# Two transformer blocks on one core: another way to sum the modulation over the partitions

## The chip, the cores and the metric

The kernel runs on one core of a Trainium2 chip. The metric is device time in microseconds (us) of one execution, the median of several; lower is better. A core has a matmul engine (TensorE, PE in the profile), three elementwise engines (VectorE or DVE, ScalarE or ACT, GpSimd or POOL), and queues that start DMAs; here nearly all of them are issued on the queue of SyncE (SP), in the order of the program. Every engine works through its own instructions in order and waits for the others by semaphores.

## What is computed

Two transformer blocks on 256 tokens of width 1024, in float32. The first is a mixer (gated convolution and forgetting attention) and a SwiGLU layer. The second has two layers, each an attention and a SwiGLU layer, and each of the four is wrapped in a modulation that is worked out from one vector `c`:

```python
c_act = silu(c)                               # 1 x 1024
for i in range(2):
    mod = c_act @ ada_w[i] + ada_b[i]         # 1024 x 6144
    sh_a, sc_a, g_a, sh_f, sc_f, g_f = split(mod, 6)
    h = rms_norm(x, norm_g[i, 0]) * (1 + sc_a) + sh_a
    y = attention_i(h)
    x = x + g_a * rms_norm(y, norm_g[i, 1])
    h = rms_norm(x, norm_g[i, 2]) * (1 + sc_f) + sh_f
    x = x + g_f * rms_norm(swiglu(h), norm_g[i, 3])
```

The change concerns the last step of `c_act @ ada_w[i]` alone: twelve vectors of 1024 values.

## The kernel before

All 256 tokens stay in the core's on-chip memory, and 227 MB of weights stream through it once. A weight tile of 128x512 is split into two parts (`hi`, a rounded copy written by ScalarE, and `lo`, the rest, written by VectorE, in `fill`, lines 331 to 360), and each product of weights and tokens is three matmuls (`triple`, lines 385 to 395): hi by hi, hi by lo, lo by hi. Weights arrive in 3 buffers `raw` of 1 MB each; split tiles wait in 16 pairs (`slots`), and in the SwiGLU layers in 8 more (`wp`). Each split tile of a SwiGLU layer feeds 6 matmuls.

The order of all instructions on each engine is written out when the program is built. `Order` (line 111) is a small planner: it keeps a clock `now` that advances with each matmul (`mm`, `tr`), and lanes for the other engines with estimated costs (`Lane`, line 77). Side work is written as generators that are spawned and resumed when the planner's clock reaches the time that they yielded. `pin` (line 127) then fixes each engine's order. Real waits are by semaphores, so an instruction whose input comes later than planned holds up all that is behind it on its engine or queue.

The modulation is side work of this kind. `ada` (lines 659 to 690) goes through 12 vectors (`ada_order`) in two halves `cc` of 512 columns, 4 loads of 512 KB each (`araw`). For each half, 8 VectorE instructions multiply a 128x512 tile of weights by a value per partition and add it to a tile `asum` (2 buffers), which also gets the bias in its first row. What is then left is a sum over the 128 partitions, by `ada_finish` (lines 626 to 657), in one of two ways:

- Shifts and scales (`sh`, `sc`; 8 vectors, 16 halves) are wanted with the channel on the partition, as `fm`. PE turns the tile in four 128x128 pieces, VectorE sums each row out of PSUM (`reduce_sum`, 512 values per partition); for a scale a second small VectorE instruction adds 1 and multiplies by the norm's gain.
- Gates (`g`; 4 vectors, 8 halves) are wanted on all partitions, as a row of 1024. Before, a tile `gain` is loaded with the norm's gain, the same row on all partitions (`load_gain`). The sum is split into hi and lo (ScalarE, VectorE), two matmuls with a matrix of ones give it on all partitions, and VectorE multiplies `gain` by it. There are 2 `gain` tiles, shared with the norms of the first block; `ada_finish` waits until its tile has been loaded, and holds its `asum` until then.

The users are `chain` (line 555: it waits for `gb.marks`, the gate, and `ready`, shift and scale) and `evacuate`. At the start, `rows` (line 447) loads the small vectors as rows into one tile, each by a DMA of its own on SP, after the loads of `x` and the first weights and ahead of all further weights (lines 483 to 490); `turn_rows` turns them all by one PE instruction into the tile `cols`. `small` allocates one tile each; `pad_end` is one that nothing reads.

Of the kernel before, what the change touches and what calls it, by code (L numbers as in the profile page):

```python
# [12 lines left out]
F32 = mybir.dt.float32  # L13
F32R = mybir.dt.float32r
AF = mybir.ActivationFunctionType
OP = mybir.AluOpType
AX = mybir.AxisListType
# [3 lines left out]
P = 128  # L21
D = 1024
# [11 lines left out]
STOCK = 9  # L34
ADA_START, ADA_EARLY, ADA_LATE = 30.0, 5.5, 8.0
HEADS_1, HEADS_2 = 9.0, 2.0
PAD_END = 104
FIRST_DMA, SLOW_BYTES = 1.9, 2.2e6
RATE, SLOW_RATE = 360e3, 270e3
WARM = 6  # L40
# [178 lines left out]
def block_kernel(ctx: ExitStack, tc: tile.TileContext, a: dict, onehot: bass.AP, out: bass.AP):  # L219
    nc = tc.nc  # L220
    o = Order(tc)
    A, V, G = o.A, o.V, o.G
# [4 lines left out]
    dram = ctx.enter_context(tc.tile_pool(name="dram", bufs=1, space=DRAM))  # L227

    def ring(pool, name, n, shape, dtype=F32):
        return Ring([pool.tile(shape, dtype, name=f"{name}{i}") for i in range(n)])  # L230

    def small(name, shape, dtype=F32):
        return cst.tile(shape, dtype, name=name)

    banks = ring(psum, "bank", 8, [P, 512])
    raws = ring(cst, "raw", 3, [P, 2048])
    araws = ring(cst, "araw", 2, [P, 1024])
    slots = Ring([(small(f"hi{i}", [P, 512], F32R), small(f"lo{i}", [P, 512], F32R)) for i in range(16)])
    st = ring(cst, "st", 4, [P, 528])
    ch = ring(cst, "ch", 3, [P, 512])  # L240
    ep = ring(cst, "ep", 4, [P, 384])
    gains = ring(cst, "gain", 2, [P, D])
    asum = ring(cst, "asum", 2, [P, 512])
    junk = small("junk", [P, 512], mybir.dt.bfloat16)
    tiny = [small(f"tiny{i}", [P, 4]) for i in range(40)]
    tiny_at = [0]

    def tiny_tile():
# [113 lines left out]
    def split(hi, lo, src, after=0.0):  # L362
        t = A.activation(hi, src, AF.Copy, after=after)
        return V.tensor_sub(lo, src, hi.bitcast(F32), after=t)
# [80 lines left out]
    vec = {}  # L445
# [29 lines left out]
    def stay_warm():  # L475

        b = banks.take()
        for _ in range(WARM):
# [8 lines left out]
    later = rows(("c", a["c_2"].rearrange("l (k p) -> (l k) p", p=P), 8),  # L487
                 ("conv", a["conv_w"].rearrange("l t (k p) -> (l t k) p", p=P), 12),
                 ("ffn_pre", a["norm_ffn_pre"].rearrange("l (k p) -> (l k) p", p=P), 8),
                 *((("g", l, i), a["norm_g_2"][l, i].rearrange("(k p) -> k p", p=P), 8) for l in range(2) for i in (0, 2)))  # L490
    ident = small("ident", [P, P])
    make_identity(nc, ident)
    tri = small("tri", [P, P])
    nc.vector.memset(tri, 1.0)
    ones_r = small("ones_r", [P, P], F32R)
# [114 lines left out]
    def load_gain(src, gain):  # L610
        gain.tile = yield from o.get(gains)
        gain.load.t = o.dma(gain.tile, src.to_broadcast([P, D]))


    fm = [small(f"fm{l}", [P, 4, 8]) for l in range(2)]
# [3 lines left out]
    ada_done = {one: [Mark(), Mark()] for one in ada_order}  # L619
    gated = {one: Gain() for one in ada_order if one[1][0] == "g"}  # L620
# [2 lines left out]
    c_mark = Mark()  # L623
    c_act = small("c_act", [P, 8])

    def ada_finish(l, what, cc, sums, r):
        yield r
        c = slice(cc * 512, (cc + 1) * 512)
        if what[0] == "g":
            yield from o.until(gated[l, what].load)  # L630
            pair = yield from o.get(slots)
            hv, lv = pair
            r = split(hv, lv, sums)
            asum.give(sums, r)
            yield r
            tp = yield from o.get(banks)
            o.mm(tp, ones_r, hv, True, False)
            r = o.mm(tp, ones_r, lv, False, True)
            slots.give(pair, r)
            yield r  # L640
            dst = gated[l, what].tile[:, c]
            r = V.tensor_mul(dst, dst, tp)
        else:
            tp = yield from o.get(banks)
            for j in range(4):
                r = o.tr(tp[:, j * P:(j + 1) * P], sums[:, j * P:(j + 1) * P], ident)
            asum.give(sums, r)
            yield r
            i = {"sh_a": 0, "sc_a": 1, "sh_f": 2, "sc_f": 3}[what]
            dst = fm[l][:, i, cc * 4:cc * 4 + 4]  # L650
            r = V.reduce_sum(dst, tp.rearrange("p (k c) -> p k c", c=P), axis=AX.X)
            if what[1] == "c":
                yield r
                g = vec["g", l, 0 if what == "sc_a" else 2][:, cc * 4:cc * 4 + 4]
                r = V.scalar_tensor_tensor(dst, dst, 1.0, g, op0=OP.add, op1=OP.mult)
        banks.give(tp, r)
        ada_done[l, what][cc].t = r

    def ada():
        yield from o.until(c_mark)  # L660
        pieces = [(l, what, cc, k0) for l, what in ada_order for cc in range(2) for k0 in range(0, 8, 2)]
        loaded, t0 = [], o.now
        for i in range(len(pieces) + 1):
            if i < len(pieces):
                l, what, cc, k0 = pieces[i]
                c0 = parts_of.index(what) * D + cc * 512
                if k0 == 0:
                    if what[0] == "g" and cc == 0:
                        o.spawn(load_gain(a["norm_g_2"][l, 1 if what == "g_a" else 3].unsqueeze(0), gated[l, what]))
                    sums = yield from o.get(asum)  # L670
                    r = G.memset(sums, 0.0)
                    yield r
                    ba = o.dma(sums[0:1, :], a["ada_b_2"][l:l + 1, c0:c0 + 512])
                t = yield from o.get(araws)
                arrival = o.dma(t.rearrange("p (k c) -> p k c", c=512),
                                a["ada_w_2"][l].rearrange("(k p) c -> p k c", p=P)[:, k0:k0 + 2, c0:c0 + 512])
                loaded.append((l, what, cc, k0, t, max(arrival, ba), sums))
            if i:
                l, what, cc, k0, t, arrival, s = loaded.pop(0)
                yield max(arrival, t0 + i * ADA_EARLY)  # L680
                while (o.urgent or V.free > o.now + SLACK or
                       pos["lo"] - pos["first"] < STOCK and o.now < t0 + i * ADA_LATE):
                    yield o.now + 0.2
                for k in range(2):
                    r = V.scalar_tensor_tensor(s, t[:, k * 512:(k + 1) * 512], c_act[:, k0 + k:k0 + k + 1], s,
                                               op0=OP.mult, op1=OP.add)
                    yield r - 0.3
                araws.give(t, r)
                if k0 == 6:
                    o.spawn(ada_finish(l, what, cc, s, r), r)  # L690


    def scope(**kinds):

        stack, got = ExitStack(), {}
        for name, (n, shape, dtype) in kinds.items():
            got[name] = ring(stack.enter_context(tc.tile_pool(name=name, bufs=1, reuse_waits="tile")), name, n, shape, dtype)
        return stack, got
# [87 lines left out]
    cum, cum_mark = [small(f"cum{h}", [P, 8]) for h in range(2)], [Mark(), Mark()]  # L786
    rows_mark = Mark()

    small("pad_end", [P, PAD_END])
    phase, sc = scope(qp=(4, [P, 4, 256], F32), gp=(8, [P, 512], F32),  # L790
                                   mk=(1, [P, 256], F32))
    qks, gp = sc["qp"], sc["gp"]
# [209 lines left out]
    group(take(2), 260, keep_gb, None)  # L1002
    o.spawn(gates_of_c())
    o.spawn(ada(), ADA_START)
    group(take(2), 512, keep_gc, None)
    group(take(2), 512, make_z, None)
# [392 lines left out]
```

## Time and profile before

| | us |
|---|---|
| median of 3 runs (985.66 to 992.59) | 987.0 |
| the profiled execution, its own time | 987.64 |
| its span, first to last instruction | 985.9 |
| PE busy | 976.0 (99%) |
| VectorE busy | 739.6 (75%) |
| ScalarE busy | 605.1 (61%) |
| GpSimd busy | 35.4 (4%) |
| DMA queue of the weights, share of 16 engines | 67.9% |

The span is what the trace covers; 1.7 us of the execution lie around it. Durations of neighbouring instructions on one engine overlap in the records, on PE and on VectorE: what one more instruction costs its engine is the distance from start to start, not its duration.

### The profile page before, as it was taken

What the parts mean: (1) busy time and instruction counts of PE and PEld (TensorE: products, weight loads), DVE (VectorE), ACT (ScalarE), POOL (GpSimd) and SP (SyncE); (2) the same over time, 40 slices, a digit from 0 to 9 for tenths busy, and PEclk for the clock granted to TensorE, in tenths of its full rate; (3) what the DMA queues carried; (4) which work ended last, traced back from release to release, by engine and by line L of the source; (5) the groups of instructions that cost most, each with busy time, mean ns of one, the idle gap of its engine ahead of it and who ended that gap; (6) DMA issues with size and microseconds to landing.
All of it is one profiled execution on the core that took longest, in us unless ns stands there. A gap on an engine that the chain in (4) does not pass through costs nothing.

```text
span 985.9 us, 14069 instructions
## 1 busy us (share of the span) xinstructions
PE 976.0 (99%) x4826; PEld 805.9 (82%) x4826; DVE 739.6 (75%) x1470; ACT 605.1 (61%) x1286; POOL 35.4 (4%) x65
## 2 busy tenths in 40 slices
PE   9999999999999999999999999999999999999997
PEld 6888778888888878898888888888897888888885
DVE  6789789989888868887899888637766796464632
ACT  7756675765546437866775554537878785454631
POOL 1000000000000001000000000001000100000000
PEclk9999999999999999999999999999999999999999
DMA  7977777679988874784779989636542657556401
GB/s 244 345 240 263 258 281 238 232 226 344 349 279 303 300 272 170 270 297 153 243 223 324 349 287 322 224 106 222 180 137 82 198 196 261 200 166 206 161 22 44
DMA packets 143637, 227.22 MB, mean 230 GB/s; under 512 B 6087, under 2 KB 79028, under 8 KB 143564
## 3 DMA queue, kind: packets, MB, share of 16 engines
q1 hardware_dynamic: 143548, 226.30, 67.9%
q8 instruction: 38, 0.62, 0.3%
q14 instruction: 35, 0.29, 0.1%
q10 hardware_dynamic: 16, 0.00, 0.0%
HBM read 225.22 MB, written 2.63 MB: 231 GB/s over the span
## 4 chain that ended last, share of the span: by engine, by line
PE 90%; DMA 3%; DVE 3%; issue 2%; ACT 1%; SPq 0%; POOL 0%; DVEq 0%; POOLq 0%; ACTq 0%
PE bank L145 85%; PE bank L151 5%; DMA araw<-in_ada_w_dram 2%; DVE asum L89 1%; DVE lo L89 1%; DMA x<-in_x_dram 1%; DVE wp L89 0%; ACT hi L89 0%; SPq L137 0%; DMA raw<-in_w_in_dram 0%; DVE x L89 0%; DVE ch L89 0%; ACT junk L89 0%; POOL tiny L89 0%; ACT L89 0%
## 5 line engine op out<-in xcount | busy, mean ns | idle before, releaser
L89 DVE TENSOR_TENSOR lo<-raw,hi 128x512 fp32r<-128x512 f32 (+1 forms) x499 | 322.9, 677 | 35.8 <-ACT hi L89 34.1
L89 ACT ACTIVATE hi<-raw 128x512 fp32r<-128x512 f32 (+1 forms) x499 | 298.0, 621 | 59.8 <-PE bank L145 35.2
L145 PE MATMUL bank<-hi,hTh 128*128 128x512 f32 (+1 forms) x670 | 262.7, 392 | 0.5 <-ACT hTh L89 0.5
L145 PE MATMUL bank<-hi,hTl 128*128 128x512 f32 (+1 forms) x670 | 261.8, 391 | 0.2 <-DVE hTl L89 0.2
L145 PE MATMUL bank<-lo,hTh 128*128 128x512 f32 (+1 forms) x670 | 261.0, 389 | 0.0
L145 PE MATMUL bank<-hi,pair 128*128 128x512 f32 x528 | 173.5, 394 | 0.0
L89 DVE SCALAR_TENSOR_TENSOR asum<-araw,c_act,asum 128x512 f32<-128x512 f32 x192 | 143.3, 746 | 7.9 <-DMA araw<-in_ada_w_dram 7.2
L145 PEld LDWEIGHTS bank<-hi,hTl 128*128 128x128 f32 x670 | 125.9, 188 | 26.1 <-issue 1.3
L145 PEld LDWEIGHTS bank<-lo,hTh 128*128 128x128 f32 x670 | 126.0, 188 | 24.2 <-DVE lo L89 0.8
L145 PEld LDWEIGHTS bank<-hi,hTh 128*128 128x128 f32 x670 | 125.9, 188 | 24.2 <-ACT hTh L89 1.3
L145 PE MATMUL bank<-wp,hTh 128*128 128x512 f32 x388 | 120.4, 391 | 0.0
L145 PEld LDWEIGHTS bank<-hi,pair 128*128 128x128 f32 x528 | 98.0, 188 | 19.7 <-issue 0.2
L89 ACT ACTIVATE ep<-bank 128x256 f32<-128x256 f32 x66 | 25.4, 384 | 131.8 <-PE bank L145 131.3
L145 PE MATMUL bank<-lo,pair 128*128 128x512 f32 x264 | 103.6, 393 | 0.0
L89 ACT ACTIVATE wp<-raw 128x512 fp32r<-128x512 f32 x145 | 88.9, 630 | 22.4 <-PE bank L145 16.4
L89 DVE TENSOR_TENSOR wp<-raw,wp 128x512 fp32r<-128x512 f32 x145 | 95.2, 686 | 8.8 <-ACT wp L89 8.6
L145 PEld LDWEIGHTS bank<-wp,hTh 128*128 128x128 f32 x388 | 72.5, 188 | 15.1
L89 DVE TENSOR_TENSOR ep<-ep,bank 128x256 f32<-128x256 f32 x70 | 29.2, 417 | 66.7 <-ACT ep L89 66.4
L145 PE MATMUL bank<-wp,hTl 128*128 128x512 f32 x194 | 75.9, 391 | 0.0
L145 PE MATMUL bank<-wp,pair 128*128 128x512 f32 x288 | 75.8, 396 | 0.0
L145 PEld LDWEIGHTS bank<-wp,pair 128*128 128x128 f32 x288 | 53.0, 188 | 10.4
L89 DVE TENSOR_TENSOR pair<-bank,pair 128x256 fp32r<-128x256 f32 (+1 forms) x74 | 32.5, 439 | 37.3 <-ACT pair L89 36.7
(131 smaller groups left out, 953.6 us busy)
## 6 DMA issues: line engine op xcount, KB each, us to landing
araw<-in_ada_w_dram SPq DMA_DIRECT2D x96, 512.0 KB
raw<-in_ffn_w_in_dram SPq DMA_DIRECT2D x88, 512.0 KB
raw<-in_w_gate_up_dram SPq DMA_DIRECT2D x44, 512.0 KB
raw<-in_ffn_w_out_dram SPq DMA_DIRECT2D x22, 1024.0 KB
raw<-in_w_in_dram SPq DMA_DIRECT2D x16, 1024.0 KB
raw<-in_moba_w_qkv_dram SPq DMA_DIRECT2D x12, 1024.0 KB
raw<-in_diff_w_qkv_dram SPq DMA_DIRECT2D x12, 1024.0 KB
raw<-in_w_down_dram SPq DMA_DIRECT2D x11, 1024.0 KB
```

Source lines behind the costliest of these rows:

```text
L89: self.order.pin(self, fn(out, *args, **kw))
L145: self.pin(self.pe, self.nc.tensor.matmul(out, lhsT, rhs, start=start, stop=stop, skip_group_check=shared))
L151: self.pin(self.pe, self.nc.tensor.transpose(out, src, ident))
```

## The change

`ada_finish` no longer uses two ways. For each half, VectorE turns the 128x512 tile in blocks of 32x32 (`V.transpose`) into a tile `z`, and sums each row of each block (`reduce_sum`, 512 values per partition into 16), into one half of a tile `fold` of 128x32. After the second half, four float32 matmuls, with a stationary tile `stacked` of 128x32 (four 32x32 identities above each other) and 8 moving columns, give the vector's 1024 values as 128x8. For a shift VectorE copies them, for a scale it does the one instruction with 1 and the gain, for all 1024 values at once. For a gate it multiplies them by the norm's gain (128x8, loaded at the start with the other small vectors), the 128x8 go to DRAM by a DMA and come back on all partitions by another, into a `gain` tile that is only taken then. The gain loads ahead of a gate go. `tiny` has 36 instead of 40 buffers and `pad_end` goes.

```diff
-PAD_END = 104
-    tiny = [small(f"tiny{i}", [P, 4]) for i in range(40)]
+    tiny = [small(f"tiny{i}", [P, 4]) for i in range(36)]
...
-                 *((("g", l, i), a["norm_g_2"][l, i].rearrange("(k p) -> k p", p=P), 8) for l in range(2) for i in (0, 2)))
+                 *((("g", l, i), a["norm_g_2"][l, i].rearrange("(k p) -> k p", p=P), 8) for l in range(2) for i in range(4)))
     ident = small("ident", [P, P])
     make_identity(nc, ident)
+    stacked = small("stacked", [P, 32])
+    for q in range(4):
+        nc.vector.tensor_copy(stacked[q * 32:(q + 1) * 32], ident[q * 32:(q + 1) * 32, q * 32:(q + 1) * 32])
...
+    folded = Ring([(small(f"fold{i}", [P, 32]), Mark(), Mark()) for i in range(2)])
+    fold_of, gate = {}, small("gate", [P, 8])
+    gate_d = dram.tile([4, D], F32, name="gate_d")
+
     def ada_finish(l, what, cc, sums, r):
-        yield r
-        c = slice(cc * 512, (cc + 1) * 512)
+        yield r
+        if not cc:
+            fold_of[l, what] = yield from o.get(folded)
+            for m in fold_of[l, what][1:]:
+                m.t = None
+        while (l, what) not in fold_of:
+            yield o.now + 0.1
+        one = fold_of[l, what]
+        z = yield from o.get(st)
+        r = V.transpose(z[:, :512], sums)
+        asum.give(sums, r)
+        yield r
+        r = V.reduce_sum(one[0][:, cc * 16:(cc + 1) * 16], z[:, :512].rearrange("p (b j) -> p b j", j=32), axis=AX.X)
+        st.give(z, r)
+        one[1 + cc].t = r
+        if not cc:
+            return
+        yield from o.until(*one[1:])
+        tp = yield from o.get(banks)
+        for q in range(4):
+            r = o.mm(tp[q * 32:(q + 1) * 32, :8], stacked, one[0].rearrange("p (k q) -> p q k", q=4)[:, q], True, True)
+        folded.give(one, r)
+        yield r
         if what[0] == "g":
-            yield from o.until(gated[l, what].load)
-            pair = yield from o.get(slots)
-            hv, lv = pair
-            r = split(hv, lv, sums)
-            asum.give(sums, r)
-            yield r
-            tp = yield from o.get(banks)
-            o.mm(tp, ones_r, hv, True, False)
-            r = o.mm(tp, ones_r, lv, False, True)
-            slots.give(pair, r)
-            yield r
-            dst = gated[l, what].tile[:, c]
-            r = V.tensor_mul(dst, dst, tp)
+            i = (0 if what == "g_a" else 1) + 2 * l
+            r = V.tensor_mul(gate, tp[:, :8], vec["g", l, 1 if what == "g_a" else 3])
+            banks.give(tp, r)
+            yield r
+            yield o.dma(gate_d[i:i + 1].rearrange("o (k p) -> p (o k)", p=P), gate) + 1.0
+            gain = gated[l, what]
+            gain.tile = yield from o.get(gains)
+            r = o.dma(gain.tile, gate_d[i:i + 1].to_broadcast([P, D]))
         else:
-            tp = yield from o.get(banks)
-            for j in range(4):
-                r = o.tr(tp[:, j * P:(j + 1) * P], sums[:, j * P:(j + 1) * P], ident)
-            asum.give(sums, r)
-            yield r
             i = {"sh_a": 0, "sc_a": 1, "sh_f": 2, "sc_f": 3}[what]
-            dst = fm[l][:, i, cc * 4:cc * 4 + 4]
-            r = V.reduce_sum(dst, tp.rearrange("p (k c) -> p k c", c=P), axis=AX.X)
             if what[1] == "c":
-                yield r
-                g = vec["g", l, 0 if what == "sc_a" else 2][:, cc * 4:cc * 4 + 4]
-                r = V.scalar_tensor_tensor(dst, dst, 1.0, g, op0=OP.add, op1=OP.mult)
-        banks.give(tp, r)
-        ada_done[l, what][cc].t = r
+                r = V.scalar_tensor_tensor(fm[l][:, i], tp[:, :8], 1.0, vec["g", l, 0 if what == "sc_a" else 2],
+                                           op0=OP.add, op1=OP.mult)
+            else:
+                r = V.tensor_copy(fm[l][:, i], tp[:, :8])
+            banks.give(tp, r)
+        for m in ada_done[l, what]:
+            m.t = r
...
-                    if what[0] == "g" and cc == 0:
-                        o.spawn(load_gain(a["norm_g_2"][l, 1 if what == "g_a" else 3].unsqueeze(0), gated[l, what]))
...
-    small("pad_end", [P, PAD_END])
```

## Rows read from the trace of the kernel before

**Rows 1.** The page: busy time of each engine, share of the span, instructions.

```profile
PE 976.0 (99%) x4826; PEld 805.9 (82%) x4826; DVE 739.6 (75%) x1470; ACT 605.1 (61%) x1286; POOL 35.4 (4%) x65
```

**Rows 2.** The page: chain of work that ended last, by engine.

```profile
PE 90%; DMA 3%; DVE 3%; issue 2%; ACT 1%; SPq 0%; POOL 0%; DVEq 0%; POOLq 0%; ACTq 0%
```

**Rows 3.** Chain in order of time, one piece: start us, us, what.

```profile
835.57 10.48 PE bank L145 x46
```

**Rows 4.** Groups by form, PE: instruction, out<-in, shapes, count | busy us, mean ns.

```profile
L145 PE MATMUL bank<-hi,hTh 128*128 128x512 f32 x638 | 253.7, 398 | 0.5 <-ACT hTh L89 0.5
...
L151 PE MATMUL bank<-ident,asum 128*128 128x128 f32 x64 | 9.6, 273 | 0.5 <-DVE asum L89 0.5
...
L145 PE MATMUL bank<-hi,ones_r 128*128 128x512 f32 x8 | 3.2, 394 | 0.0
```

**Rows 5.** Timeline of PE, 68 to 69.2: start us, us, instruction.

```profile
68.21 0.39 PE L145 MATMUL bank<-hi,hTl 128*128 128x512 f32 x1
68.44 0.60 PE L151 MATMUL bank<-ident,asum 128*128 128x128 f32 x4
...
69.11 0.40 PE L145 MATMUL bank<-lo,hTh 128*128 128x512 f32 x1
```

**Rows 6.** Timeline of PE, 39 to 40: start us, us, instruction.

```profile
39.13 0.28 PE L145 MATMUL bank<-logf,ones_r 128*128 128x8 f32 x2
39.27 0.37 PE L145 MATMUL bank<-logf,tri 128*128 128x8 f32 x2
39.49 0.47 PE L145 MATMUL bank<-hi,hTl 128*128 128x512 f32 x1
39.80 0.39 PE L145 MATMUL bank<-hi,hTh 128*128 128x512 f32 x1
```

**Rows 7.** Groups by form, weight loads of PE (PEld) of three widths.

```profile
L145 PEld LDWEIGHTS bank<-logf,tri 128*128 128x128 f32 x4 | 0.6, 190 | 0.9 <-issue 0.9
...
L145 PEld LDWEIGHTS bank<-ep,gp 128*64 128x64 f32 x32 | 3.3, 136 | 3.6 <-issue 0.7 <-DVE lo L89 0.7 <-DVE ep L89 0.4
...
L145 PEld LDWEIGHTS bank<-st,tab 33*8 33x8 f32 x2 | 0.1, 84 | 0.4 <-issue 0.4
```

**Rows 8.** Groups by form, VectorE: instructions of the modulation's last step.

```profile
L89 DVE TENSOR_REDUCE fm<-bank 128x4 f32<-128x512 f32 x16 | 11.0, 688 | 5.1 <-PE bank L151 5.0
...
L89 DVE TENSOR_TENSOR lo<-asum,hi 128x512 fp32r<-128x512 f32 x8 | 5.5, 690 | 4.6 <-ACT hi L89 4.6
...
L89 DVE TENSOR_TENSOR gain<-gain,bank 128x512 f32<-128x512 f32 x8 | 5.4, 679 | 0.2 <-PE bank L145 0.2
```

**Rows 9.** Timeline of VectorE, two weight splits back to back.

```profile
250.94 1.29 DVE L89 TENSOR_TENSOR lo<-raw,hi 128x512 fp32r<-128x512 f32 x2
```

**Rows 10.** Windows: stretch, its us, busy PE, PEld, DVE, ACT, POOL, clock, DMA.

```profile
210.00:260.00 50.00, 50.00 (x233) 41.08 (x233) 47.87 (x84) 26.26 (x52) 1.58 (x3) 1.00 0.98 340
```

**Rows 11.** Timeline of SP's queue, 7 to 10: small rows, then weights.

```profile
7.05 2.30 SPq L137 DMA_DIRECT2D ep<-in_norm_g_dram  x4
9.68 2.81 SPq L137 DMA_DIRECT2D raw<-in_w_in_dram  x6
```

**Rows 12.** Timeline of ScalarE and PE, 12 to 15.

```profile
12.43 0.63 ACT L89 ACTIVATE hi<-raw 128x512 fp32r<-128x512 f32 x1 [0.70 <-DMA raw<-in_w_in_dram]
...
14.04 0.50 PE L145 MATMUL bank<-hi,hTh 128*128 128x512 f32 x1 [0.50 <-ACT hTh L89]
```

**Rows 13.** Windows of the start and of the end.

```profile
8.00:9.70 1.70, 1.56 (x8) 0.89 (x8) 1.70 (x5) 1.49 (x3) 0.00 (x0) 1.00 0.28 97
...
980.00:982.00 2.00, 0.00 (x0) 0.00 (x0) 1.28 (x3) 0.62 (x2) 0.55 (x1) 1.00 0.01 4
982.00:984.00 2.00, 0.00 (x0) 0.00 (x0) 0.89 (x2) 0.00 (x0) 0.00 (x0) 1.00 0.46 170
```

**Rows 14.** Waits of SP's queue: who for whom, us in total, times, longest.

```profile
SPq L137 <- DVE lo L89: 341.7, 107, 18.2
```

**Rows 15.** The page: DMA queue of the weights, packets, MB, share of 16 engines.

```profile
q1 hardware_dynamic: 143548, 226.30, 67.9%
```

## The prediction

> **What bounds the kernel now.** I read the page's busy times first, then its chain of waits, then the timeline of PE from end to end for distances between starts, and only then the engines that the change touches. PE is busy 976.0 of 985.9 us [rows 1], but matmul records overlap (a 512-column product shows 398 ns [rows 4]), so the share alone proves little. The chain says more: 90% of what ended last is PE [rows 2], and in a long stretch 46 products follow each other in 10.48 us, 0.228 us each [rows 3]. PE's idle time is 985.9 - 976.0 = 9.9 us [rows 1], and at least four of these lie behind its last product [rows 13]; in between, the timeline of PE shows few gaps that aren't the cost of switching from one form of matmul to another. So the kernel is bound by the number of PE instructions and by when PE gets going: an instruction less on PE is time won, and one more, or a hole, is time lost. VectorE has 25% to spare on average, but not everywhere: from 210 to 260 it is busy 47.87 of 50 us [rows 10].
>
> **PE: what goes.** Sixteen halves (shifts and scales) lose their block of four turns. From the product before such a block to the second one after it the starts are 0.90 us apart (68.21 to 69.11 [rows 5]); two plain steps would be 0.46, so a block costs 0.44 us, of which some 0.08 is the slower step after it. 16 x 0.44 = 7.0 us. Eight gate halves lose two products with ones; in their form they are like any other [rows 4]: 16 x 0.228 = 3.65 us. Together 10.7 us of PE, all on the path.
>
> **PE: what comes.** Twelve blocks of four float32 products with 8 columns. The nearest rows are the products with `logf` [rows 6], also float32 with 8 moving columns: each is recorded as two instructions, so a block has eight. With full-width weights a pair takes 0.14 us from start to start where its weights were loaded during a wait, 0.22 where they were not, and the next plain step is 0.08 longer. That is 0.07 to 0.11 per instruction. Those weights have 128 columns, `stacked` has 32, and weight loads shorten with width: 190 ns at 128, 136 at 64, 84 at 8 [rows 7], 0.87 ns per column. Upper bound: 8 x 0.11 + 0.08 = 0.96 us a block, 11.5 us for twelve. Lower bound: if only the width counts, 0.11 x 32/128 = 0.028 per instruction, 8 x 0.028 + 0.08 = 0.30, 3.6 us. I take 0.06 per instruction, a little under the 0.07 that is a row: 8 x 0.06 + 0.08 = 0.56, 6.7 us. PE's net is 6.7 - 10.7 = -4.0 us, with ends -7.1 and +0.8.
>
> **The start.** Four more small vectors are loaded on SP, ahead of the second weight buffer. The four of that form before take from 7.05 to 9.68 [rows 11], 0.66 us each, though the DMA engines are nearly idle there (share 0.28 [rows 13]): it is SP's own pace, not a full queue. So the weight loads that begin at 9.68 would begin 4 x 0.66 = 2.6 us later. ScalarE already waits for the first of them at 12.43, and PE at 14.04 for a ScalarE instruction behind that one [rows 12]. ScalarE works in order, so PE's restart moves from 14.04 to about 16.6. Nothing later gives that back, since PE is the bound from there on: +2.6 us. The high end is 2.8; the low end is 0.4 (0.27 us each, the duration of one issue, less the 0.7 us that PE idles there already). A hole of 3.3 us need not cost clock: at the end PE has nothing for four us and the granted clock stays at 1.00, the 2.4 GHz level [rows 13]. The four VectorE copies into `stacked` fall where VectorE waits for `x`; if that cover went they would cost under 1 us, once.
>
> **VectorE, ScalarE, buffers.** Removed from VectorE: 16 row sums, 8 `lo` and 8 products with `gain`, each near 0.69 us by its record [rows 8]. Two such instructions back to back take 1.29 us together [rows 9], so one costs 0.60: 32 x 0.60 = 19.2, and 8 small ones bring it to 20. Added: 24 turns, 24 sums, 12 small instructions. The turn is in no row. Its bounds are half of a 128x512 instruction (0.3) and two passes (1.2); I take 0.60, like all others of that size. 24 x 1.20 + 12 x 0.1 = 30. VectorE gets 10 us more (3 to 25) over the whole modulation, and I cost that at nothing, since the planner starts a multiplication only when it sees VectorE free, and the split weights in stock feed PE meanwhile. The cover is thin from 210 to 260, where three vectors end and VectorE has 2.1 us free in 50 [rows 10]; there it may become a wait of PE. ScalarE loses 8 splits, which is not on the path. Gates no longer hold `asum` until a `gain` tile is free, so the later multiplications come earlier; what is late next is then the planner's own spacing of 5.5 us per load. For all such shifts in the order I add +1.0 us of PE waits (0 to 5).
>
> **The gates' way via DRAM.** Each gate adds to SP's queue a store of 128x8 and a broadcast load, and loses a broadcast load of the same size. The store waits for one small VectorE instruction, the load for the store to land; behind both on SP stand the weight loads, and for those wait ScalarE and VectorE, then PE. The store writes 1,024 values of 4 bytes, each 512 bytes from the next. A packet of the weights' queue takes 0.679 x 16 x 985.9 / 143,548 = 75 ns of one engine [rows 15]. If each value were such a packet, a store would take 1,024 x 75 / 16 = 4.8 us on 16 engines, four of them 19 us. I cost it at nothing: SP spends a third of the span waiting for VectorE to free a weight buffer (341.7 us [rows 14]), so weights mostly lie ready, three buffers of 4 tiles and up to 16 split ones, and a tile feeds 6 x 0.228 = 1.4 us of PE; 5 us late is 4 tiles of stock.
>
> A rule speaks against this: the Trainium skill, DMA: Bandwidth & Descriptors, section Rules for kernel authors, says that a last dimension which is not contiguous is lowered to one descriptor per element. By it the store would be 1,024 descriptors, which is the case just priced; no store of this form is in the trace, so it neither agrees nor disagrees.
>
> **The sum.** -4.0 + 2.6 + 1.0 = -0.4 us. The profiled execution took 987.64, so 987.2; that lies 0.2 above the median of the runs shown (987.0), and well within their spread of 7 us. A measurement of this kernel can tell about 1% (9.9 us) from no change, so the forecast is no change. Its own range is from -7.1 + 0.4 + 0 to +0.8 + 2.8 + 5, or 980.9 to 996.2.
>
> **Rivals.**
>
> *A. Narrow products are nearly free and the early loads are mostly hidden.* -10.7 + 3.6 + 0.4 = -6.7: 980.9. For it: weight loads shorten with width [rows 7]. Against: a row as short as 0.03 per instruction isn't in the trace, and SP's pace of 0.66 held four times. Chance 0.22.
>
> *B. SP's queue is held by the stores (the other side: slower).* A store lands 4.8 us after its issue at the earliest if each value is a packet, and some 2.7 us more pass as for any load (9.68 to 12.43 [rows 11, 12]); SP stands for 7.5 us, four times, and where the stock of split tiles is under 7.5 / 1.4 = 5 to 6, PE stands as well. If that holds at all four, 30 us: 987.2 - 1.0 + 30 = 1016. It decides from a landing of some 7 us with less than 6 tiles in stock. The descriptor rule cited above is what makes a packet of each value. Against it: a queue that stands for its buffers a third of the span has room for 30 us of other waits. Chance 0.06.
>
> *C. VectorE becomes the bound where it is full.* All of its 10 us on the path: 987.2 - 1.0 + 10 = 996; with a turn of two passes, 25 us: 1011. For it: 47.87 of 50 busy [rows 10]. Against: only some stretches are full, and the multiplications give way. Chance 0.10, half of it above 1%.
>
> *D. The float32 products cost what full width costs.* +0.8 + 2.6 + 1.0 = +4.4: 992.0. The change then doesn't relieve PE: that would be the case in which it doesn't do what it says. For it: the 0.22 of [rows 6]. Chance 0.12.
>
> **Chances.** The forecast has 0.50, A 0.22, D 0.12, C 0.10, B 0.06. The range 981 to 996 holds the forecast, A, D and half of C, some 0.85 with its edges counted. Faster by over 1% needs more than all of PE's removed work, or some shift in the order that takes out waits as well: 0.06. Slower by over 1%: B, half of C and a little for other holes in a new order: 0.13. The rest, 0.81, is within 1%.
>
> **What would show it.** Each step has its place in the profile after. PE: no turns of `asum`, no `ones_r` of 512 columns; 96 records with `stacked`, 12 blocks, 0.56 us from the step before to the step after beyond plain steps. Start: eight `norm_g` loads on SP, the next weights at about 12.3 and PE's restart at 16.6. VectorE: about 10 us more busy, a turn 0.60 from start to start. SP: behind each gate store a wait for its landing of under 6 us, with no PE wait after it. The prediction is wrong if PE shows waits of more than 5 us in all after 20 us (then B or C, by the releaser: a DMA or VectorE), if a block costs 1 us (D) or 0.3 (A), or if the second weight loads start before 10.5.

## The result: 2.6% slower, and the profile after

The changed kernel takes 1013.0 us (1011.5 to 1018.0 in 4 runs), the kernel before beside it 986.7. The ratio is 1.0261, with a 95% interval of 1.0233 to 1.0289. That is outside the predicted range (981 to 996) and on the side that had 0.13. The profiled execution has a span of 1009.8 us against 985.9.

The page of the changed kernel: busy time by engine, the chain by engine, and the waits of SP's queue for the stores:

```profile
PE 988.0 (98%) x4842; PEld 803.0 (80%) x4842; DVE 751.0 (74%) x1494; ACT 596.0 (59%) x1278; POOL 34.8 (3%) x65
...
PE 86%; DMA 5%; DVE 3%; issue 2%; ACT 2%; SPq 0%; POOL 0%; DVEq 0%; POOLq 0%; ACTq 0%
...
SPq L136 <- DMA gate_d<-gate: 18.7, 3, 7.6
```

Beside [rows 1, 2]: PE has only 16 records more (turns and products with ones went, 96 small ones came), but is busy 12 us longer, and 5% of the chain are DMAs instead of 3%. Two things are behind it. The first is in one row, the same stretch of a SwiGLU layer as [rows 3], in the chain in order of time of the changed kernel:

```profile
925.70 10.69 PE bank L144 x46
```

The same 46 products take 10.69 us instead of 10.48. Over the whole span the mean step from start to start of two neighbouring products of 512 columns is 0.2325 us where it was 0.2280. The first 50 us have it already (0.2302 instead of 0.2261), before the first of the new products runs at 102. The trace has some 3,260 such steps; times 0.0045 that is 14.7 us.

The second is at three of the four gates. In SP's queue around the second gate, `gate_d<-gate` is the store and `gain<-gate_d` the load that brings the gate back:

```profile
463.00 0.37 SPq L136 DMA_DIRECT2D gate_d<-gate  x1
463.64 0.37 SPq L136 DMA_DIRECT2D raw<-in_moba_w_o_dram  x1
466.01 1.02 SPq L136 DMA_DIRECT2D raw<-in_ffn_w_in_dram  x2
474.65 0.34 SPq L136 DMA_DIRECT2D gain<-gate_d  x1
```

PE there, in the timeline of the same kernel (what it waited for stands in brackets):

```profile
473.05 0.38 PE L144 MATMUL bank<-ptp,gp 128*128 128x128 f32 x2
478.25 3.36 PE L144 MATMUL bank<-ptp,gp 128*128 128x128 f32 x14 [4.81 <-ACT gp L88]
```

The chain in order of time there:

```profile
463.64 12.84 DMA raw<-in_moba_w_o_dram
476.48 0.02 issue
476.50 0.02 ACTq L88
476.52 0.04 issue
476.56 0.13 ACT hi L88
```

Windows of 2 us there (busy PE, PEld, DVE, ACT, POOL, then granted clock, DMA share, GB/s):

```profile
472.00:474.00 2.00, 1.43 (x8) 1.01 (x6) 1.96 (x4) 0.00 (x0) 0.00 (x0) 1.00 0.83 129
474.00:476.00 2.00, 0.00 (x0) 0.00 (x0) 0.17 (x1) 0.00 (x0) 0.00 (x0) 0.97 0.78 209
476.00:478.00 2.00, 0.00 (x0) 0.00 (x0) 0.00 (x0) 1.44 (x3) 0.00 (x0) 0.50 1.08 337
480.00:482.00 2.00, 2.00 (x10) 1.90 (x10) 0.00 (x0) 0.36 (x1) 0.00 (x0) 0.50 1.06 388
482.00:484.00 2.00, 2.00 (x9) 1.60 (x8) 1.73 (x3) 2.00 (x5) 0.00 (x0) 0.83 1.10 351
484.00:486.00 2.00, 2.00 (x11) 1.60 (x10) 2.00 (x4) 1.43 (x3) 0.00 (x0) 1.00 0.71 254
```

The store is issued at 463.00. The weight load right behind it takes 12.84 us to land; the load that brings the gate back can be issued only at 474.65. ScalarE waits for those weights with a copy behind them (`gp`) for which PE waits 4.81 us, and by then the granted clock is down to a half, the 1.2 GHz level: 14 small products take 3.36 us. The chain at the other two names loads of `araw`, VectorE in the middle and turns of PE at the end. At the third gate:

```profile
618.37 10.20 DMA araw<-in_ada_w_dram
628.66 0.75 DVE asum L88
```

VectorE stands for that load with a small instruction behind it (`ep`), and PE waits for `ep`. So at none of the gates does PE wait for split weights. It waits 2.60 and 0.79 us after the first gate and 3.24 after the third, 11.4 us with the second.

### The profile page after: what moved, and what is told of

It reads as the page before. It is cut to its first block, busy times and chain, and to the rows that moved or that the text cites. A ratio compares the mean times of both kernels' runs of the same rounds, so it can differ in the third digit from the quotient of the medians.

```text
span 1009.8 us, 14122 instructions
## 1 busy us (share of the span) xinstructions
PE 988.0 (98%) x4842; PEld 803.0 (80%) x4842; DVE 751.0 (74%) x1494; ACT 596.0 (59%) x1278; POOL 34.8 (3%) x65
## 4 chain that ended last, share of the span: by engine, by line
PE 86%; DMA 5%; DVE 3%; issue 2%; ACT 2%; SPq 0%; POOL 0%; DVEq 0%; POOLq 0%; ACTq 0%
PE bank L144 82%; PE bank L150 4%; DMA araw<-in_ada_w_dram 3%; DMA raw<-in_moba_w_o_dram 1%; DVE asum L88 1%; ACT hi L88 1%; DVE lo L88 1%; DMA bf<-in_b_f_dram 1%; DMA x<-in_x_dram 0%; DVE wp L88 0%; SPq L136 0%; ACT junk L88 0%; DMA raw<-in_w_in_dram 0%; DVE x L88 0%; DVE st L88 0%
## 5 line engine op out<-in xcount | busy, mean ns | idle before, releaser
L88 ACT ACTIVATE hi<-raw 128x512 fp32r<-128x512 f32 (+1 forms) x494 | 293.1, 619 | 78.2 <-PE bank L144 40.8
L144 PE MATMUL bank<-hi,hTh 128*128 128x512 f32 (+1 forms) x652 | 257.7, 395 | 1.5 <-ACT hTh L88 1.5
L144 PE MATMUL bank<-hi,hTl 128*128 128x512 f32 (+1 forms) x652 | 257.4, 395 | 0.1
L144 PE MATMUL bank<-hi,pair 128*128 128x512 f32 x544 | 179.6, 398 | 0.0
L144 PE MATMUL bank<-wp,hTh 128*128 128x512 f32 x424 | 134.7, 397 | 0.0
L144 PE MATMUL bank<-lo,pair 128*128 128x512 f32 x272 | 108.7, 400 | 0.0
L144 PEld LDWEIGHTS bank<-wp,hTh 128*128 128x128 f32 x424 | 79.3, 188 | 17.7
L144 PE MATMUL bank<-wp,hTl 128*128 128x512 f32 x212 | 83.9, 396 | 0.0
L88 ACT ACTIVATE pair<-bank 128x256 fp32r<-128x256 f32 (+1 forms) x74 | 29.0, 392 | 65.9 <-PE bank L150 55.8
L144 PE MATMUL bank<-wp,pair 128*128 128x512 f32 x264 | 67.6, 398 | 0.0
```

The costliest lines, as they stand in the source:

```text
L88: self.order.pin(self, fn(out, *args, **kw))
L144: self.pin(self.pe, self.nc.tensor.matmul(out, lhsT, rhs, start=start, stop=stop, skip_group_check=shared))
```

## The experiments

The theory after that profile has two parts. One is about places: `tiny` has 4 buffers less, and `stacked`, `fold` and `gate` are allocated further back, so `pair`, `x`, `hTh` and `hTl` lie 128 bytes lower in each partition. (Addresses stand in no trace. They are worked out here from the order and the sizes of the allocations, with 32 bytes for a buffer of `tiny`, whose 4 values take 16; `e1`, which puts a tile of 128 bytes in the place of four of them, bears that out.) Of these, `pair`, `hTh` and `hTl` are the stationary operands of the products, and the step of those is what changed. The other is about the store of 1,024 single values. Rivals: something else in the program slows PE; SP's wait for the store is the price, not the store; VectorE is full.

### The places alone

**The kernel before, with these tiles moved** (`e2`). The program is the same, instruction for instruction:

```diff
-    tiny = [small(f"tiny{i}", [P, 4]) for i in range(40)]
+    tiny = [small(f"tiny{i}", [P, 4]) for i in range(36)]
...
     hT = (small("hTh", [P, NKT, 256], F32R), small("hTl", [P, NKT, 256], F32R))
+    tiny += [small(f"tiny{i}", [P, 4]) for i in range(36, 40)]
```

> The kernel before with one edit: 4 of its 40 small buffers are allocated behind hTl instead of ahead of pair. The program is the same; only pair, x, hTh and hTl lie 128 bytes lower, as in the changed kernel. Theory of the addresses: the step of a 512-column product rises from 0.2284 to 0.2325 us, the time from 987 to about 1002. Rival: step and time as before, 987 within 3 us.

Measured: 1000.05 us (999.9 to 1001.9), before 987.98; ratio 1.0128 (1.0109 to 1.0148). Its chain:

```profile
948.21 10.69 PE bank L145 x46
```

The row of the changed kernel, from a kernel in which only addresses differ. The mean step is 0.2325. So moving four groups of tiles alone costs the kernel before 12 us.

**The changed kernel, with these tiles back** (`e1`):

```diff
     tiny = [small(f"tiny{i}", [P, 4]) for i in range(36)]
+    stacked = small("stacked", [P, 32])
...
     make_identity(nc, ident)
-    stacked = small("stacked", [P, 32])
```

> The changed kernel with one edit: the tile stacked (128 bytes per partition) is allocated right behind the 36 small buffers, where 4 more of them were before. So pair, x, hTh and hTl lie at the addresses that they had in the kernel before; nothing else in the program differs. Theory (the 128 bytes by which these tiles moved set the step of PE): a 512-column product goes back from 0.2325 to 0.2284 us from start to start, 3,570 of them give 15 us, so about 998. Rival (something else in the new program slows PE, such as its small DMA packets or the new form of matmul): the step stays at 0.2325 and the time at 1013.

Measured: 1003.4 us (1001.0 to 1007.5); ratio 1.0163 (1.0131 to 1.0194). The step is back, a mean of 0.2278; the same products in its chain:

```profile
956.98 10.46 PE bank L144 x46
```

The gain, 9.6 us, is less than the 15 expected. The trace, of the slowest of the four runs (1007.5), has longer waits of PE at the gates: 1.11, 0.30, 4.70, 4.73 and 3.75 us, 14.6 in all instead of 11.4. The likely reason, which no run isolates, is that a faster PE comes to the gates earlier and stands longer for the same late loads. This way round the two costs don't simply add.

### Which distance counts

Most products have `pair`, `hTh` or `hTl` as stationary and `hi`, `lo` or `wp` as moving operand. In the kernel before all of them begin at the same place modulo 256 bytes; which place that is doesn't matter for what follows. Three runs of the kernel before, with other splits of the same 40 buffers, move one side, the other, or a part (single runs, read by the step):

```diff
 e6, and e7 with the last 4 behind hTl:
+    tiny = [small(f"tiny{i}", [P, 4]) for i in range(4)]
     slots = Ring([(small(f"hi{i}", [P, 512], F32R), small(f"lo{i}", [P, 512], F32R)) for i in range(16)])
...
-    tiny = [small(f"tiny{i}", [P, 4]) for i in range(40)]
+    tiny += [small(f"tiny{i}", [P, 4]) for i in range(4, 40)]
 e8: 36 ahead of pair, and
     pairs = ring(cst, "pair", 4, [P, 4, 256], F32R)
+    tiny += [small(f"tiny{i}", [P, 4]) for i in range(36, 40)]
```

> The kernel before with one edit: 4 of the small buffers are allocated ahead of hi0, 36 behind junk. All hi and lo tiles (the moving operand of most products) and what lies behind them up to junk move up by 128 bytes; pair, x, hTh, hTl and the wp tiles stay. If the step is set by the place of the stationary tile alone (pair, hTh, hTl): 0.2284 everywhere and 987. If by the place of the moving tile: 0.2325 for hi and lo, 0.2284 for wp, about 998. If by the distance of the two from each other: the same as the last, 0.2325 for hi and lo only, and in the next run 0.2284 for them.

> The kernel before; hi and lo lie 128 bytes higher and pair, x, hTh and hTl 128 bytes lower, so both begin at a multiple of 256 bytes; wp stays at 128 over one. By the distance of the two: 0.2284 for products of hi and lo, 0.2325 for those of wp, about 990. By the stationary tile alone: 0.2325 everywhere, 1000. By each of them by itself: over 0.2325 for hi and lo.

> The kernel before; only the four pair tiles lie 128 bytes lower, hTh, hTl and x stay. Pair is stationary in 1,080 of the 3,592 products of 512 columns, hTh and hTl in the rest. If the place of a product's own operands sets its step: 0.2325 for products with pair and 0.2284 for those with hTh and hTl, about 991. If something else moved with the tiles (x, or the order in which they lie): all at 0.2284, 987, or all at 0.2325, 1000.

Two more keep the moving tiles and put the stationary ones 256 and 64 bytes lower (32 or 38 buffers ahead of `pair`, the rest behind `hTl`):

> The kernel before; pair, x, hTh and hTl lie 256 bytes lower instead of 128 (8 small buffers behind hTl). If what counts is the distance of the stationary tile from the moving one within 256 bytes: 0.2284 us a step and 987. If it counts within a longer stretch, or any move away from the old places costs: 0.2325 and 1000.

> The kernel before; pair, x, hTh and hTl lie 64 bytes lower (2 small buffers behind hTl). If the cost comes only when the two tiles are half of 256 bytes apart: 0.2284 and 987. If every distance but none at all costs the same: 0.2325 and 1000. If it grows with the distance: about 0.2305, some 993.

Measured; the step is the mean from start to start of neighbouring products of that kind (those above 0.27 us, where another form of matmul lies between, are left out), and the distance is between the starts of the two tiles, modulo 256, worked out as above:

| run | us | distance to `hi`, `lo` | step | distance to `wp` | step with `hTh` |
|---|---|---|---|---|---|
| before | 987 to 988 | 0 | 0.2280 | 0 | 0.2275 |
| `e2`, stationary 128 lower | 1000.05 | 128 | 0.2325 | 128 | 0.2325 |
| `e6`, `hi` and `lo` 128 higher | 998.31 | 128 | 0.2325 | 0 | 0.2292 |
| `e7`, both | 991.96 | 0 | 0.2286 | 128 | 0.2319 |
| `e8`, `pair` only | 993.34 | 128 with `pair`, 0 with `hTh` | 0.2324, 0.2282 | 0 | 0.2279 |
| `e9`, stationary 256 lower | 987.02 | 0 | 0.2280 | 0 | 0.2275 |
| `e10`, stationary 64 lower | 992.11 | 64 lower | 0.2293 | 64 lower | 0.2286 |

The chain's row for the 46 products in `e6`:

```profile
946.75 10.65 PE bank L145 x46
```

in `e9`:

```profile
936.14 10.48 PE bank L145 x46
```

and in `e10`:

```profile
940.97 10.54 PE bank L145 x46
```

`e6` and `e7` decide: the same `hi` tiles, 128 bytes higher in both, are slow with `hTh` in its old place and fast with `hTh` 128 lower, while `wp`, which didn't move, goes the opposite way. So it is neither tile's place by itself but the distance of the two. `e8` shows that only the products of the stationary tile that moved are slower. At 256 the cost is gone. At 64 the mean has 0.0013 of the 0.0045 us that 128 costs, under a third; a cost that grows evenly with the distance would be half (0.2303). But the products with `hTl` alone have just that, 0.2303, and those with `hTh` 0.2289, so how the cost grows between 0 and 128 stays open. The time of `e10` (992.1, beside a run of the kernel before at 991.9) can't tell. Products of 256 columns with the weights as stationary operand go slightly the other way: 0.1196 us before, 0.1188 in `e2`. Why the distance counts isn't shown by these runs.

### The stores

**The gate's load planned later** (`e3`):

```diff
-            yield o.dma(gate_d[i:i + 1].rearrange("o (k p) -> p (o k)", p=P), gate) + 1.0
+            yield o.dma(gate_d[i:i + 1].rearrange("o (k p) -> p (o k)", p=P), gate) + 13.0
```

> The changed kernel; the planner waits 13 us instead of 1 us between a gate's store and the load that brings it back, so that SP no longer stands for the store with weight loads behind it. Theory 1 (the store of 1,024 single values takes the DMA engines themselves: 83 GB/s in the 6 us after one, 350 and more elsewhere): weight loads issued behind the store still land some 10 us late, PE still waits at two or three gates for several us, and the time falls by less than 6 us, to 1007 or more. Theory 2 (SP's wait for the store is the cost): PE's waits near the gates go, and with them its stretches at half clock, 12 to 16 us: 997 to 1001. The step of PE stays at 0.2325 by both.

Measured: 1012.8 us (1012.1 to 1013.2); ratio 1.0252 (1.0234 to 1.0270). SP's queue no longer stands, and PE's wait is there all the same. SP in the timeline of `e3`, at the second gate:

```profile
463.17 0.37 SPq L136 DMA_DIRECT2D gate_d<-gate  x1
463.81 0.37 SPq L136 DMA_DIRECT2D raw<-in_moba_w_o_dram  x1
...
487.77 0.50 SPq L136 DMA_DIRECT2D gain<-gate_d  x1
```

its chain there:

```profile
463.81 12.76 DMA raw<-in_moba_w_o_dram
```

and PE in its timeline:

```profile
478.33 3.36 PE L144 MATMUL bank<-ptp,gp 128*128 128x128 f32 x14 [4.73 <-ACT gp L88]
```

The load back is now 24 us behind the store, and the weight load behind the store still takes 12.76 us. SP's wait for the store (18.7 us in the changed kernel) cost next to nothing; the loads issued behind the store are late in any case.

**The gate stored as rows** (`e4`). PE turns the 128x8 into 8x128, VectorE copies them, and 8 rows of 512 bytes are stored:

```diff
-            yield o.dma(gate_d[i:i + 1].rearrange("o (k p) -> p (o k)", p=P), gate) + 1.0
+            row = yield from o.get(st)
+            tp = yield from o.get(banks)
+            r = o.tr(tp[:8, :P], gate, ident)
+            yield r
+            r = V.tensor_copy(row[:8, :P], tp[:8, :P])
+            banks.give(tp, r)
+            yield r
+            r = o.dma(gate_d[i:i + 1].rearrange("o (k p) -> (o k) p", p=P), row[:8, :P])
+            st.give(row, r)
+            yield r + 1.0
```

> The changed kernel; a gate of 128x8 is turned once more by PE into 8x128, copied by VectorE, and stored as 8 rows of 512 bytes instead of 1,024 single values. Adds 4 turns on PE, 4 copies on VectorE (under 2 us of PE). Theory (the store by single values holds the DMA engines, and so weights, PE and its clock): PE's waits of 3 to 5 us at the gates go, the granted clock stays at 1.00, the time falls by 12 to 16 us to 997 to 1001; the load behind a store is issued within 4 us of it instead of 9 to 12. Rival (the waits at the gates come from VectorE being full, or from the new order): the waits stay where they are and the time at 1010 or more.

Measured: 996.6 us (996.0 to 997.1); ratio 1.0089 (1.0068 to 1.0110). 16.4 us less than the changed kernel, a little over the 12 to 16 expected, although it adds work. The window of 6 us behind the first gate (last two columns: share of the DMA engines and GB/s), in the changed kernel:

```profile
318.00:324.00 6.00, 6.00 (x28) 4.77 (x26) 3.19 (x6) 4.66 (x9) 0.00 (x0) 1.00 0.95 83
```

and in this one, with the 40 us around its second gate:

```profile
318.00:324.00 6.00, 6.00 (x29) 4.85 (x28) 5.69 (x10) 5.25 (x10) 0.00 (x0) 1.00 0.78 261
...
460.00:500.00 40.00, 40.00 (x191) 32.76 (x189) 33.60 (x62) 26.20 (x56) 2.86 (x5) 1.00 0.75 250
```

SP at that gate, in the timeline of `e4`:

```profile
461.73 0.29 SPq L136 DMA_DIRECT2D gate_d<-st  x1
...
467.86 0.34 SPq L136 DMA_DIRECT2D gain<-gate_d  x1
```

With single values the DMA engines move 83 GB/s; with rows they move 261 GB/s in the same stretch. From 460 to 500 PE has no hole and the clock stays at 1.00. One expectation failed: the load back is 7.4 and 6.1 us behind its store at the first two gates, not 4 (2.1 at the third). It stands behind weight loads and, for up to 3.3 us, for the store, and PE doesn't wait for it.

The edit also shifted the order on SP: at the second gate the weight load, right behind the store before (463.64 after 463.00), is now issued ahead of it (460.53 before 461.73). So a rival is that the order did it, and not the rows. The fourth gate tells, where in both kernels the store is followed by the same load of 1 MB. Its windows from 2 to 8 us behind the store, in the changed kernel and in `e4`:

```profile
653.90:659.90 6.00, 6.00 (x29) 4.85 (x28) 3.98 (x8) 3.39 (x7) 0.00 (x0) 1.00 0.19 16
641.20:647.20 6.00, 6.00 (x29) 4.85 (x28) 3.65 (x7) 3.34 (x7) 0.00 (x0) 1.00 0.91 338
```

With the same order it is 16 GB/s with single values and 338 with rows, and the packets of that load end 11 us after its issue (654.65) instead of 4 (639.77). PE has no hole there in either. So the form of the store is what holds the loads up. How it does so isn't shown. The page of the changed kernel has 4,224 packets more on the weights' queue than [rows 15] (over 4 x 1,024; `e4` has 128 more):

```profile
q1 hardware_dynamic: 147772, 226.34, 68.5%
```

The packets of 4 bytes are recorded with 9 ns each, which would be 0.6 us for 1,024 on 16 engines (an estimate). The time is in the packets of the loads: of those with 1,024 bytes that begin in the 6 us window behind the first gate, the mean is 191 ns in the changed kernel and 48 in `e4`. And at the fourth gate the engines show only a share of 0.19 while a load is outstanding.

### Both

**The version that has both mends** (`e5`: the edits of `e1` and `e4`).

> The changed kernel with both mends: stacked allocated ahead of pair, so that pair, x, hTh and hTl lie where they lay before, and the gate stored as 8 rows of 512 bytes. Theory (the places cost 12 to 16 us, the stores 16, and the rest of the change is worth its 6 us of PE less some 3 at the start and in new waits): 981 to 985, a step of 0.2284 us, no wait of PE over 1.5 us after 20 us, clock 1.00 to the end; faster than before by 0.3 to 0.7%. Rival (a third cost, which the two hid): 988 or more.

Measured: 983.2 us (981.6 to 987.4, 9 runs) against 988.4 (14 runs); ratio 0.9946 (0.9929 to 0.9963). Its page:

```profile
PE 971.0 (99%) x4846; PEld 799.9 (82%) x4846; DVE 750.9 (77%) x1498; ACT 595.2 (61%) x1278; POOL 34.8 (4%) x65
```

PE is busy 5 us less than in [rows 1], with steps of 0.2279. Behind the start its longest wait is 0.64 us, at 494. The expectation had the clock at 1.00 to the end; the profile's mean is 0.997, mostly because of a stretch near the start, behind a wait of PE of 1.81 us:

```profile
18.00:20.00 2.00, 2.00 (x6) 1.59 (x5) 2.00 (x7) 2.00 (x8) 0.00 (x0) 0.50 0.88 248
```

It beats the kernel before by half a percent and the changed one by 2.9%. From here the loss can be laid out: 988.4 - 5.2 (the change as meant), + 13.4 (places, 983.2 to 996.6), + 16.4 (stores, 996.6 to 1013.0). That it closes is no proof, since each step is the difference of two runs; taken the other way, by `e1`, it is 20.2 for the stores and 9.6 for the places.

## Why the prediction was wrong

**What bounds the kernel: right, but not complete.** PE's instructions and PE's holes are the time, and every part of the result is one of the two. What it lacks is that the length of an unchanged instruction can change as well as the number.

**PE, what goes and comes: right in sign, mis-sized by 2 us.** The small products are cheaper than I took. The timeline of PE at the first block:

```profile
102.07 0.39 PE L144 MATMUL bank<-hi,hTh 128*128 128x512 f32 x1
102.39 0.25 PE L144 MATMUL bank<-fold,stacked 128*32 128x8 f32 x8
102.57 0.50 PE L144 MATMUL bank<-lo,hTh 128*128 128x512 f32 x1
102.91 0.39 PE L144 MATMUL bank<-hi,hTl 128*128 128x512 f32 x1
```

From 102.07 to 102.91 there are 0.84 us; two plain steps are 0.465, so a block costs 0.38 instead of 0.56. The eight instructions take 0.18, 0.022 each, below my lower bound of 0.028; switching to them and back takes the other 0.2, of which I had counted 0.08. Twelve blocks, the others much like this one: 4.5 us instead of 6.7, PE's net -6.2 instead of -4.0. Rival A was nearer with its 3.6, rival D falls. `e5` shows the change where little covers it: -5.2 us in all, with what the start costs.

**PE, the step of 0.228 us: the step that failed first.** I took it from [rows 3] as a constant. It holds for one distance between the tiles, and the change moves the stationary ones by 128 bytes through a line of the diff (`tiny`, 40 to 36) that I gave no cost at all. No row of the kernel before could have priced it, but the diff said that allocations moved, and 3,592 products of one form are the place where 0.004 us matters.

**The start: mis-sized, at 2.6 us.** SP's eight small loads and the weight loads behind them, in the timeline of the changed kernel:

```profile
6.49 3.86 SPq L136 DMA_DIRECT2D ep<-in_norm_g_dram  x8
10.39 11.26 SPq L136 DMA_DIRECT2D raw<-in_w_in_dram  x9
```

PE's restart there:

```profile
14.80 0.50 PE L144 MATMUL bank<-hi,hTh 128*128 128x512 f32 x1 [1.49 <-ACT hTh L88]
```

0.48 us for each, not 0.66, and the first begins earlier than in [rows 11]. The weights are 0.7 us later and PE's restart is at 14.80 instead of 14.04 [rows 12]: +0.8 instead of +2.6. 10.39 lies before the 10.5 that I had named as a sign of being wrong. Other runs of the changed order have the restart at 14.69 (`e4`) to 15.89 (`e3`), at most +1.9. The way it takes (SP, weights, ScalarE, PE) is as forecast.

**VectorE: right.** It is busy 11.4 us more (10 forecast); a turn has a mean of 704 ns and a sum 679, like others of that size, and the full stretches cost PE next to nothing: with rows stored (`e4`, `e5`) no wait of PE behind the start is over 0.75 us. At the first and third gates PE waits for VectorE, which I had named as the sign of rival C, but VectorE stands there for a late load itself. Rival C falls.

**The gates: the second step that failed.** I priced the store at 4.8 us from the mean packet, saw one descriptor per value as the case in question, and then cost it at nothing, because SP has time to spare and there are split weights in stock. Both reasons missed what happened. At the first three gates it was 9 to 12 us from the store's issue to the load that waits for it, and the loads behind it moved at a third of their pace meanwhile (83 against 261 GB/s); on the chain, loads issued from 0.7 us ahead of a store to 4.9 us behind it take 10.20 to 12.84 us to land. And the stock of split weights is no cover here, because PE didn't wait for weights but for small instructions of ScalarE and VectorE (`gp`, `ep`) that stood behind those late loads. The rule weighed there is one descriptor per element (the Trainium skill, DMA: Bandwidth & Descriptors, section Rules for kernel authors). The trace agrees: there are 4,224 packets more on the queue, over the 4 x 1,024 values. Rival B, which rests on one packet per value, gave 1016, close to what came, but that is half chance: its mechanism was SP's wait, which `e3` shows to cost next to nothing, and about half of the loss was the step. It had PE stand at gates, and PE does so at three of four, but not for want of split tiles.

**The clock: wrong by its reason.** I argued from [rows 13] that a hole need not cost clock. In the changed kernel that held at the start, where PE waited 1.49 us; in `e3` and `e5`, with waits of 1.75 and 1.81 us there, the clock then was at a half for 3.4 us. And after the wait at the second gate PE ran at half clock until 482.7, and after that at the third for 3.4 us. At the third gate:

```profile
634.00:636.00 2.00, 2.00 (x6) 1.61 (x5) 1.59 (x4) 0.71 (x3) 0.00 (x0) 0.50 1.11 354
```

These are some 7.8 us of work at half clock, so they cost 3.9 us (an estimate): most of what the 16.4 us are beyond the 11.4 us of waits.

## What to carry to other kernels

Before costing an edit on PE's path, look whether it moves a tile: with thousands of equal products, the distance between stationary and moving tile modulo 256 bytes is worth 9.6 to 13.4 us here, and two lines of allocation decide it. Count the contiguous pieces of a DMA, and look for its price at the loads behind it and at what stands for those, not only at the queue that issues it: here four stores of 4 KB in 1,024 pieces cost about three times what the change could win (16.4 us against 5.2). Where a changed kernel is slower by more than its parts explain, compare a row that should not have changed at all.

## What was not expected of the hardware

- The step of a 512-column product in this form: 0.228 us when stationary and moving tile begin at the same place modulo 256 bytes, 0.2325 at a distance of 128, about 0.229 at 64, 0.228 again at 256 (`e2`, `e6` to `e10`). Why isn't shown.
- Four float32 products with 32 stationary columns and 8 moving ones, recorded as eight instructions, take 0.18 us; the two switches around them take as much again.
- Behind a store of 1,024 values of 4 bytes each the DMA engines moved 83 GB/s over 6 us at the first gate and 16 at the fourth; behind the same 4 KB as 8 rows of 512 bytes, 261 and 338. The small packets are recorded with 9 ns each; the weight packets behind them are what takes longer.
